# Moving the last tile's transposes into the first plain block, and fixing VectorE's order there, in a one-core diffusion layer

## The chip, the cores and the metric

The kernel runs on one core of a Trainium2 chip. The metric is the device time of one execution in microseconds (us). Before the change the median of three runs is 766.42 us (765.01 to 767.63). One core has a matrix engine (TensorE, "PE" in the profile; its weight loads are "PEld"), VectorE ("DVE"), ScalarE ("ACT"), GpSimd ("POOL") and SyncE ("SP"), which here only issues DMAs.

## What is computed

One layer of a hybrid backbone on 640 tokens: 128 context tokens and 512 latent tokens, model width 1024. Cut to what matters, for each of the two token kinds with its own conditioning vector:

```
mod = silu(cond) @ w_ada + b_ada           # six vectors: sh1, sc1, g1, sh2, sc2, g2
h   = rms(x) * (1 + sc1) + sh1
proj = h @ w_in                            # q, k, v and three conv inputs
mix = concat(rms(attention), rms(conv mixer)) @ w_out
x   = x + g1 * mix
h2  = rms(x) * (1 + sc2) + sh2             # <- the change is here
gate, up = split(h2 @ w_gate_up)           # 1024 -> 2 x 2816
x   = x + g2 * ((silu(gate) * up) @ w_down)
```

All is float32. Each float32 product is made of three matmuls in a faster format: an operand is split into a rounded part "hi" (a copy by ScalarE) and a remainder "lo" (a subtraction by VectorE), and hi·hi + hi·lo + lo·hi is accumulated.

## The kernel before

The tokens lie in five tiles of 128, in the order TORD: context, then latent tiles 0 to 3. TensorE's instructions run in program order (a manual schedule for that engine alone). The other engines' orders are made at build time by a greedy planner, which takes ready instructions by priority; a priority is the place in the program, moved ahead by `early(n)` or behind by a negative n. The order that it makes is then fixed on each engine's queue.

**Output projection** (lines 1040 to 1105). For each half j of the 1024 output columns, and each token tile, 24 matmuls into two PSUM accumulators, one for attention and one for the conv mixer. With j = 0 the tile's result gets its two row scales (L1079 on ScalarE, L1080 on VectorE), then is multiplied by g1 (L1082) and added to x (L1083); these two run on GpSimd for the first PX = 2 tiles, on VectorE for the others. ScalarE then squares the sum with accumulation along the row (L1095), and VectorE makes a mean (L1098). With j = 1 VectorE does the same work in four instructions (L1086 to L1090), and the second sum of squares completes the mean (L1101), GpSimd takes it to the power -1/2 (L1103), and VectorE writes the normalised tile x2n (L1105; one buffer). Beside it VectorE accumulates g2 from streamed weights (g2_step, "aacc", L989/L991), at low priority, and splits the weights of half 1 (L246 on ScalarE, L247 on VectorE). Weights come by SP's queue into three buffers "wf"; a load waits until the buffer's last reader is done.

**h2_turn(t)** (L953). Eight 128x128 transposes of x2n on TensorE (L960) into two PSUM tiles, then eight evictions with scale and shift into h2. The table H2E says how many of each four go to VectorE (L966); the others go to ScalarE (L968). For latent tile 3, the last, that is two of four. Tiles but the last are transposed inside the loop of j = 1, one tile late.

**Feed-forward.** The 22 column blocks f of w_gate_up: the first two are "plain", the others use a Strassen-like scheme with seven products in place of eight. The 640 tokens are two halves of 320, LO and HI, and h2 makes the quarters B11, B21 (LO) and B12, B22 (HI). The last tile is columns 192 to 320 of HI. A plain block on LO needs B11 and B21; on HI it needs B12 and B22. Blocks f = 2 on also need the token sums T1 to T4 (b_sums, L1028): each a subtraction of quarters (tr, L1035), ScalarE's copy (L1021) and VectorE's remainder (L1022). Before the change the order in the program is: B12 and B22 of columns 0 to 192, sums of columns 0 to 192, block 0 LO, the last tile's h2_turn, B12 and B22 of columns 192 to 320, block 1 LO, sums of columns 192 to 320, block 0 HI, block 1 HI.

**Operands of the weights** (op_load, L193). A block's g and u halves are loaded whole, and each quarter, or sum of quarters (sx, L205), is split by L149 (ScalarE) and L150 (VectorE) into a buffer "wh" or "wl", four of each, which is free again when TensorE has used it for the last time. W(key) loads up to nine entries ahead of the one that is asked for; entries of f = 2 and later have phase 3 and are held back until phase[0] is 3. Until then the stream ends with block 1's last operand.

Of the kernel before, what the change touches and what calls it, by code (L numbers as in the profile page):

```python
# [58 lines left out]
RSP = 0  # L59
G2P = -300  # L60
CRP = '0e'
H2E = [0, 0, 0, 2, 0]
PX = 2
SPO = 0
BHD = ("B21",)
TL = 1
# [3 lines left out]
PHB = 2  # L70
XP = [50, 400]
BP = 300
AP0 = 60
MXP = [300, 200, 0, 0, 0]
AWB = 2
# [14 lines left out]
def build(ctx, tc, x_prompt, x_sample, c, cache_k, cache_v, c_ctx, norm_mix, norm_ffn, w_ada, b_ada,  # L90
# [54 lines left out]
    def early(n):  # L145
        return tc.high_priority(n)
# [804 lines left out]
    TORD = [CTX] + list(range(NL))  # L951
    TS = {t: slice(n * P, (n + 1) * P) for n, t in enumerate(TORD)}

    def h2_turn(t):
        cc = 1 if t == CTX else 0
        for g in range(2):
            tp = PB((P, 4, P))
            for i in range(4):
                k = 4 * g + i
                pe.transpose(tp[:, i], x2n[t][:, k * P:(k + 1) * P], ident)  # L960
            for i in range(4):
              with early(BP):
                k = 4 * g + i
                dst, a, b = h2[g][:, i, TS[t]], modA[1][:, k, cc:cc + 1], modB[1][:, k, cc:cc + 1]
                if i >= 4 - H2E[t]:
                    dve.tensor_scalar(dst, tp[:, i], a, b, ALU.mult, ALU.add)  # L966
                else:
                    act.activation(dst, tp[:, i], AF.Identity, bias=b, scale=a)  # L968
# [71 lines left out]
    for j in range(2):  # L1040
        cols = slice(j * 512, (j + 1) * 512)
        for n, t in enumerate(TORD):
            cc = 1 if t == CTX else 0
            c0 = t * P + (2 if t == CTX else 0)
            if j == 0:
                with early(MXP[n]):
                    mixed[t] = [mix_ctx if t == CTX else mix_half(of[t]),
                                mix_half(yf[:, :, c0:c0 + P], "sx" if t == NL - 1 else "mx")]
            ms = mixed[t]
            ab = [PB(tag="h") for _ in range(2)]  # L1050
            for half in range(2):
                for p in range(4):
                    wh, wl = W(("o", j, 2 * half + p // 2))
                    mm3(ab[half], ms[half][0][:, p], ms[half][1][:, p], wh[:, p % 2], wl[:, p % 2],
                        p == 0, p == 3)
                if j == 0 and CRP == f"{n}{'me'[half]}":
                    next(ada_gen, None)
                    conv_rms()
            if j == 1 and n:
                h2_turn(TORD[n - 1])  # L1060
                with early(BP):
                    if n == 2:
                        b_plain("B11 B21", slice(0, 256))
                    if n == 3:
                        b_plain("B11 B21", slice(256, HALF))
            if j == 0 and n == 1:
                att_rms(NL - 1)
                act.activation(warm, rA[NL - 1], AF.Silu)
            if j == 0 and G2N <= n < 4 + G2N:
                g2_step(0, n - G2N)  # L1070
            if j == 1 and n == 0:
                g2_out(0)
            if j == 0:
                x2[t] = T("x2", (P, D), F32, NT)
                sp.dma_start(x2[t], x_dram[t])
            with early(XP[j]):
                m = T("mix", (P, 512), F32, 2)
                if j == 0:
                    act.activation(m, ab[0], AF.Copy, scale=rA[t])  # L1079
                    dve.scalar_tensor_tensor(m, ab[1], rB[t], m, ALU.mult, ALU.add)  # L1080
                    e = pool if n < PX else dve
                    e.tensor_tensor(m, m, g1[cc][:, cols], ALU.mult)  # L1082
                    e.tensor_tensor(x2[t][:, cols], m, x2[t][:, cols], ALU.add)  # L1083
                else:
                    with early(AP0):
                        dve.scalar_tensor_tensor(m, ab[0], rA[t], g1[cc][:, cols], ALU.mult, ALU.mult)  # L1086
                        dve.tensor_tensor(x2[t][:, cols], m, x2[t][:, cols], ALU.add)
                    m = T("mix", (P, 512), F32, 2)
                    dve.scalar_tensor_tensor(m, ab[1], rB[t], g1[cc][:, cols], ALU.mult, ALU.mult)
                    dve.tensor_tensor(x2[t][:, cols], m, x2[t][:, cols], ALU.add)  # L1090

            
            ss = T("ss", (P, 1), F32, 6)
            with early(XP[j]):
                act.activation(m, x2[t][:, cols], AF.Square, accum_out=ss)  # L1095
                if j == 0:
                    ms0[t] = T("ms0", (P, 1), F32, NT)
                    dve.tensor_scalar(ms0[t], ss, 1.0 / D, EPS, ALU.mult, ALU.add)  # L1098
                else:
                    q = T("ms", (P, 1), F32, 4)  # L1100
                    dve.tensor_scalar(q, ss, 1.0 / D, ms0[t], ALU.mult, ALU.add)  # L1101
                    r = T("rs", (P, 1), F32, 6)
                    pool.tensor_tensor(r, q, neghalf[:, :1], ALU.pow)  # L1103
                    x2n[t] = T("x2n", (P, D), F32, 1)
                    dve.tensor_scalar_mul(x2n[t], x2[t], r)  # L1105
# [16 lines left out]
        for k in range(4):  # L1122
            mm3(out[:, :HALF], w[:, 0, k], w[:, 1, k], *B[b][k], start and k == 0, stop and k == 3, more)

    def plain(f, bs, toks):

        ps = [FB(), FB()]
        for x, a in zip(ps, ("A1", "A2")):
            for i in (1, 2):
                prod(x, f, f"{a}{i}", bs[i - 1], i == 1, i == 2)  # L1130
        if toks is LO:
            st[f] = T("cg", (P, TOK), F32, 2), T("cu", (P, TOK), F32, 2)
        cg, cu = st[f]
        act.activation(cg[:, toks], ps[0][:, :HALF], AF.Silu)
        dve.tensor_tensor(cu[:, toks], ps[1][:, :HALF], cg[:, toks], ALU.mult)
        if toks is HI:
            ff_out(f, cu)
            del st[f]
# [97 lines left out]
    for gi, grp in enumerate(GROUPS):  # L1236
        for f in grp:
            if f == 0:
                two = slice(0, 192), slice(192, HALF)
                b_plain("B12 B22", two[0])  # L1240
                b_sums(two[0])
                for x in range(NPLAIN):
                    plain(x, ("B11", "B21"), LO)
                    if x == 0:
                        h2_turn(TORD[-1])
                        with early(BP):
                            b_plain("B12 B22", two[1])
                        phase[0] = 3
                b_sums(two[1])
                for x in range(NPLAIN):  # L1250
                    plain(x, ("B12", "B22"), HI)
            elif f >= NPLAIN:
                ff_a(f)
                if f - 1 in st and FEND == 1:
                    ff_end(f - 1)
                ff_c(f)
                if f - 1 in st:
                    ff_end(f - 1)
                ff_d(f)
                ff_b(f)  # L1260
                ff_e(f)
                if f == grp[-1] or FEND == 0:
                    ff_end(f)
# [55 lines left out]
```

## Time and profile before

| | us |
|---|---|
| median of three runs | 766.42 (765.01 to 767.63) |
| profiled execution, device time | 764.62 |
| its span | 762.8 |
| TensorE busy | 740.0 (97%) |
| VectorE busy | 558.8 (73%) |
| ScalarE busy | 368.8 (48%) |
| GpSimd busy | 48.9 (6%) |

The page has the busy time of each engine, the chain of work that ended last, and the costliest groups. A view of waits lists, for an engine, the line that waited, who released it, the total, the count and the longest. A timeline gives start, duration, engine, line, operation, output and inputs, shape and count of one or several merged instructions, and in brackets the idle time before and its releaser. A view by windows gives the busy time of each engine in a stretch and the TensorE clock that was granted (PEclk, 1.00 is full). Durations of neighbours overlap by pipelining. Phases of the span: input and q/k/v up to about 60 us, attention and conv to 252, output projection to 320, feed-forward to the end; within it, the plain blocks are at 321 to 356.

### The profile page before, as it was taken

To read this page: it belongs to the slowest core of one execution; us is meant where nothing else is said; L and a number is where in the kernel's file an instruction comes from. 1 tells how busy PE (TensorE), PEld (TensorE's weight loads), DVE (VectorE), ACT (ScalarE), POOL (GpSimd) and SP (SyncE) were. 2 spreads that over 40 slices of the span, in tenths; PEclk is the share of its full clock that TensorE was granted. 3 is DMA by queue.
4 is the path that set the end of the run, shared out by engine and by line. 5 is a ranking of instruction groups with operands and counts; after the bars stand their busy time and mean duration, and the time that the engine had idled before them with its cause. 6 is when DMAs were issued, how large, how long until landed. Compare 5 with 4: busy or idle time off the path is not lost.

```text
span 762.8 us, 11866 instructions
## 1 busy us (share of the span) xinstructions
PE 740.0 (97%) x4580; PEld 664.3 (87%) x4580; DVE 558.8 (73%) x1008; ACT 368.8 (48%) x711; POOL 48.9 (6%) x77
## 2 busy tenths in 40 slices
PE   4999999999999999989999999999999999999997
PEld 3678888989999876879998789998889998899986
DVE  5566987676666797888879678884578866788653
ACT  5355776666665534755552135553125541255410
POOL 3105201011010230000000000000000000000000
PEclk9999999999999999999999999999999999999999
DMA  9994134424425353031335313233113232222312
GB/s 292 303 245 132 46 107 141 123 91 125 138 90 166 119 186 111 1 111 56 93 101 175 88 56 110 70 98 111 55 56 103 64 111 77 62 85 82 111 55 83
DMA packets 102349, 84.52 MB, mean 111 GB/s; under 512 B 4526, under 2 KB 82674, under 8 KB 102292
## 3 DMA queue, kind: packets, MB, share of 16 engines
q1 hardware_dynamic: 100980, 83.39, 35.7%
q8 instruction: 36, 0.59, 0.3%
q10 hardware_dynamic: 1056, 0.26, 0.2%
q14 instruction: 21, 0.17, 0.1%
q0 software_dynamic: 256, 0.11, 0.1%
HBM read 79.68 MB, written 2.75 MB: 108 GB/s over the span
## 4 chain that ended last, share of the span: by engine, by line
PE 80%; DVE 9%; DMA 4%; issue 2%; ACT 2%; SPq 1%; POOL 1%; POOLq 0%; DVEq 0%; ACTq 0%
PE pf L153 17%; PE pf L154 17%; PE pf L155 17%; PE pc L676 3%; PE pc L677 3%; PE pc L678 3%; PE ps L790 2%; PE po L833 2%; PE pt L816 2%; PE pc L378 2%; DMA af<-in_w_ada_dram 2%; DMA wf<-in_w_gate_up_dram 1%; PE ps L153 1%; DVE aacc L991 1%; PE ph L154 1%
## 5 line engine op out<-in xcount | busy, mean ns | idle before, releaser
L149 ACT ACTIVATE wh<-wf 128x1024 fp32r<-128x1024 f32 (+1 forms) x76 | 64.1, 843 | 93.4 <-PE pf L155 63.1
L153 PE MATMUL pf<-wh,gT 128*128 128x512 f32 (+1 forms) x225 | 88.1, 392 | 0.0
L154 PE MATMUL pf<-wl,gT 128*128 128x512 f32 (+1 forms) x225 | 87.7, 390 | 0.0
L155 PE MATMUL pf<-wh,gT 128*128 128x512 f32 (+1 forms) x225 | 87.7, 390 | 0.0
L150 DVE TENSOR_TENSOR wl<-wf,wh 128x1024 fp32r<-128x1024 f32 (+1 forms) x42 | 49.4, 1175 | 28.2 <-ACT wh L149 25.3
L676 PE MATMUL pc<-hH,wh 128*128 128x320 f32 x192 | 61.1, 318 | 0.0
L677 PE MATMUL pc<-hL,wh 128*128 128x320 f32 x192 | 59.4, 310 | 0.0
L678 PE MATMUL pc<-hH,wl 128*128 128x320 f32 x192 | 59.3, 309 | 0.0
L153 PEld LDWEIGHTS pf<-wh,gT 128*128 128x128 f32 x225 | 42.2, 187 | 10.0 <-ACT wh L149 0.2
L154 PEld LDWEIGHTS pf<-wl,gT 128*128 128x128 f32 x225 | 42.2, 187 | 9.9 <-DVE wl L150 0.2
L155 PEld LDWEIGHTS pf<-wh,gT 128*128 128x128 f32 x225 | 42.2, 187 | 9.8
L153 PE MATMUL pf<-T,wh 128*128 128x320 f32 x160 | 49.6, 310 | 0.1
L154 PE MATMUL pf<-T,wl 128*128 128x320 f32 x160 | 49.5, 309 | 0.0
L155 PE MATMUL pf<-T,wh 128*128 128x320 f32 x160 | 49.5, 309 | 0.0
L154 PE MATMUL pf<-T,wh 128*128 128x320 f32 x160 | 49.5, 309 | 0.0
L155 PE MATMUL pf<-T,wl 128*128 128x320 f32 x160 | 49.5, 309 | 0.0
L153 PE MATMUL pf<-T,wl 128*128 128x320 f32 x160 | 49.5, 309 | 0.0
L153 PE MATMUL pf<-B,wl 128*128 128x320 f32 x152 | 47.3, 311 | 0.0
L154 PE MATMUL pf<-B,wl 128*128 128x320 f32 x152 | 47.1, 310 | 0.0
L155 PE MATMUL pf<-B,wl 128*128 128x320 f32 x152 | 47.1, 310 | 0.0
L1231 DVE TENSOR_TENSOR dm<-pf,g 128x512 f32<-128x512 f32 (+1 forms) x41 | 27.7, 674 | 22.9 <-PE pf L155 22.9
L149 ACT ACTIVATE wl<-wf 128x512 fp32r<-128x512 f32 x34 | 21.4, 629 | 44.7 <-PE pf L154 36.8
(297 smaller groups left out, 2052.3 us busy)
## 6 DMA issues: line engine op xcount, KB each, us to landing
wf<-in_w_gate_up_dram SPq DMA_DIRECT2D x44, 512.0 KB, 3.9
aw<-in_w_ada_dram SPq DMA_DIRECT2D x24, 512.0 KB, 4.9
wf<-in_w_down_dram SPq DMA_DIRECT2D x20, 512.0 KB, 3.4
wf<-in_w_in_dram SPq DMA_DIRECT2D x18, 512.0 KB, 5.9
af<-in_w_ada_dram SPq DMA_DIRECT2D x32, 256.0 KB, 6.0
x<-in_x_sample_dram SPq DMA_DIRECT2D x8, 512.0 KB, 4.4
wf<-in_w_out_dram SPq DMA_DIRECT2D x8, 512.0 KB, 4.6
wf<-in_w_ada_dram SPq DMA_DIRECT2D x8, 512.0 KB, 3.8
```

The costliest lines, as they stand in the source:

```text
L149: act.activation(hi, src, AF.Copy)
L150: dve.tensor_tensor(lo, src, f32(hi), ALU.subtract)
L153: pe.matmul(out, lh, rh, start=start, stop=False, skip_group_check=more)
L154: pe.matmul(out, lh, rl, start=False, stop=False, skip_group_check=more)
L155: pe.matmul(out, ll, rh, start=False, stop=stop, skip_group_check=more)
L378: pe.matmul(out[CG * g:CG * (g + 1)], cp[:, k], w, start=(k < 4), stop=(k >= KD - 4), skip_group_check=True)
L676: pe.matmul(acc, wh[:, k], hH[k][:, c0:c0 + n], start=(k == 0), stop=False)
L677: pe.matmul(acc, wh[:, k], hL[k][:, c0:c0 + n], start=False, stop=False)
L678: pe.matmul(acc, wl[:, k], hH[k][:, c0:c0 + n], start=False, stop=(k == KD - 1))
L790: pe.matmul(s2[:, g, :320], q, kk[:, v, P + g * 320:P + (g + 1) * 320], start=(i == 0), stop=(i == 1))
L816: pe.transpose(tp[:, i, h], u[3][h][:, kt * P:(kt + 1) * P], ident)
L1231: dve.tensor_tensor(dm, ps[:, :n], g2[cc][:, oc], ALU.mult)
```

## The change

- The last tile's h2_turn is called from inside plain block 0 LO, between its third and its fourth product (`mid`), with priority 1500 ahead for the evictions (BPL), and all eight evictions are on ScalarE (H2E all 0).
- B12 and B22 of columns 192 to 320 follow block 0 LO as before, with the same priority of 1500.
- The token sums are cut at column 128 in place of 192: columns 128 to 320, which hold the last tile, come first, behind the last tile's B copies; columns 0 to 128 come after block 1 LO.
- After the first part, four entries of the weight stream are loaded by hand: g and u of f = 2, its operand A11 and its operand S1. phase[0] becomes 3 only behind the second part of the sums.
- From B12/B22 of columns 0 to 192 to the second part of the sums, VectorE's instructions keep their order in the program (manual_schedule for DVE).
- PX = 0: multiply and add of the first two tiles of projection half 0 go from GpSimd to VectorE.
- The squares are taken with a scale of D^-0.5, so that the accumulated sum is the mean; L1098 falls away, and L1101 adds the two halves and epsilon.

```diff
-H2E = [0, 0, 0, 2, 0]
-PX = 2
+H2E = [0, 0, 0, 0, 0]
+PX = 0
+BPL = 1500
-    def h2_turn(t):
+    def h2_turn(t, first=None):
...
-              with early(BP):
+              with early(first or BP):
...
-            ss = T("ss", (P, 1), F32, 6)
+            ss = T("ss", (P, 1), F32, 6) if j else T("ssq", (P, 1), F32, NT)
             with early(XP[j]):
-                act.activation(m, x2[t][:, cols], AF.Square, accum_out=ss)
+                act.activation(m, x2[t][:, cols], AF.Square, scale=D ** -0.5, accum_out=ss)
                 if j == 0:
-                    ms0[t] = T("ms0", (P, 1), F32, NT)
-                    dve.tensor_scalar(ms0[t], ss, 1.0 / D, EPS, ALU.mult, ALU.add)
+                    ms0[t] = ss
                 else:
                     q = T("ms", (P, 1), F32, 4)
-                    dve.tensor_scalar(q, ss, 1.0 / D, ms0[t], ALU.mult, ALU.add)
+                    dve.tensor_scalar(q, ss, ms0[t], EPS, ALU.add, ALU.add)
...
-    def plain(f, bs, toks):
+    def plain(f, bs, toks, mid=None):
         ps = [FB(), FB()]
         for x, a in zip(ps, ("A1", "A2")):
             for i in (1, 2):
+                if mid is not None and (a, i) == ("A2", 2):
+                    mid()
                 prod(x, f, f"{a}{i}", bs[i - 1], i == 1, i == 2)
...
-                two = slice(0, 192), slice(192, HALF)
-                b_plain("B12 B22", two[0])
-                b_sums(two[0])
+                dve_order = tc.manual_schedule(engines={mybir.EngineType.DVE})
+                dve_order.__enter__()
+                b_plain("B12 B22", slice(0, 192))
                 for x in range(NPLAIN):
-                    plain(x, ("B11", "B21"), LO)
+                    plain(x, ("B11", "B21"), LO, None if x else lambda: h2_turn(TORD[-1], BPL))
                     if x == 0:
-                        h2_turn(TORD[-1])
-                        with early(BP):
-                            b_plain("B12 B22", two[1])
-                        phase[0] = 3
-                b_sums(two[1])
+                        with early(BPL):
+                            b_plain("B12 B22", slice(192, HALF))
+                        b_sums(slice(128, HALF))
+                        for _ in range(4):
+                            load_next()
+                b_sums(slice(0, 128))
+                dve_order.__exit__(None, None, None)
+                phase[0] = 3
                 for x in range(NPLAIN):
                     plain(x, ("B12", "B22"), HI)
```

## The prediction

> **What bounds the kernel now.** I read the page first, then TensorE's waits, then the timeline of each engine where a wait stands.
>
> ```profile
> span 762.8 us, 11866 instructions
> PE 740.0 (97%) x4580; PEld 664.3 (87%) x4580; DVE 558.8 (73%) x1008; ACT 368.8 (48%) x711; POOL 48.9 (6%) x77
> ...
> PE 80%; DVE 9%; DMA 4%; issue 2%; ACT 2%; SPq 1%; POOL 1%; POOLq 0%; DVEq 0%; ACTq 0%
> ```
>
> TensorE is busy for 97% and holds 80% of the chain that ended last. The change adds and takes no matmul, so it can only win where TensorE stands still or runs at a lower clock. Its waits, over the whole span, at the places that the diff touches:
>
> ```profile
> PE pf L153 <- ACT gT L1021: 3.1, 1, 3.1
> ...
> PE ph L154 <- DVE wl L247: 0.6, 2, 0.4
> ...
> PE ph L153 <- ACT wh L246: 0.5, 1, 0.5
> ...
> PE pf L154 <- DVE gT L1022: 0.3, 1, 0.3
> ```
>
> The first and the last belong to one place, the start of the second token half (HI) of the plain blocks. The middle two are in the output projection. TensorE's timeline at the first place:
>
> ```profile
> 321.30 0.40 PE L153 MATMUL pf<-B,wh 128*128 128x320 f32 x1
> ...
> 328.49 1.03 PE L960 MATMUL pt<-ident,x2n 128*128 128x128 f32 x8
> 329.28 0.40 PE L153 MATMUL pf<-B,wh 128*128 128x320 f32 x1
> ...
> 336.26 0.31 PE L155 MATMUL pf<-B,wl 128*128 128x320 f32 x1
> 339.68 0.41 PE L153 MATMUL pf<-gT,wh 128*128 128x320 f32 x1 [3.11 <-ACT gT L1021]
> ...
> 348.94 0.31 PE L153 MATMUL pf<-gT,wh 128*128 128x320 f32 x1
> ...
> 355.98 0.31 PE L153 MATMUL pf<-B,wh 128*128 128x320 f32 x1
> ...
> 357.74 0.31 PE L153 MATMUL pf<-T,wl 128*128 128x320 f32 x1
> ```
>
> Plain block 0 on the first half (LO) runs from 321.30 to 328.49 (7.19 us for four products of twelve matmuls, so 1.8 each), then come the last tile's eight transposes (0.79), then block 1 LO to about 336.4. Block 0 HI should start there; it starts at 339.68 and lasts until 348.94, which is 9.26 where its twin on the same half takes 355.98 - 348.94 = 7.04. The excess, 2.2, is a low clock beside the 0.3 wait:
>
> ```profile
> 336.41:339.68 3.27, 0.16 (x2) 0.00 (x1) 3.15 (x8) 2.92 (x8) 0.00 (x0) 1.00 0.00 0
> 339.68:344.00 4.32, 4.01 (x15) 3.78 (x16) 4.29 (x7) 1.45 (x3) 0.00 (x0) 0.60 0.00 0
> ```
>
> In these windows (length, then busy time of PE, PEld, DVE, ACT, POOL, then PEclk) TensorE stands for 3.27 us and is then granted 0.60 of its clock for 4.32 us: 0.40 x 4.32 = 1.7 lost. **The place costs 3.27 + 2.22 = 5.5 us.** What it waits for is B12 and B22 on the last tile's columns, and who is late for that stands in VectorE's timeline:
>
> ```profile
> 325.10 0.75 DVE L1105 TENSOR_SCALAR x2n<-x,rs 128x1024 f32<-128x1024 f32 x1 [0.44 <-POOL rs L1103]
> ...
> 329.91 0.95 DVE L1035 TENSOR_TENSOR tr<-gT 128x768 f32<-128x768 f32 x1
> 332.36 0.69 DVE L205 TENSOR_TENSOR sx<-wf 128x512 f32<-128x512 f32 x1 [1.50 <-DMA wf<-in_w_gate_up_dram]
> ...
> 333.84 0.95 DVE L1022 TENSOR_TENSOR T<-tr,T 128x768 fp32r<-128x768 f32 x1
> ...
> 338.18 1.36 DVE L966 TENSOR_SCALAR gT<-pt,modA,modB 128x128 f32<-128x128 f32 x4
> ...
> 341.14 0.68 DVE L1022 TENSOR_TENSOR B<-gT,B 128x512 fp32r<-128x512 f32 x1
> 342.74 0.68 DVE L1035 TENSOR_TENSOR tr<-gT 128x512 f32<-128x512 f32 x1
> ...
> 347.48 1.28 DVE L1022 TENSOR_TENSOR T<-tr,T 128x512 fp32r<-128x512 f32 x2
> ```
>
> The transposes are done by 329.3, but VectorE's half of the evictions runs at 338.18: ahead of it in VectorE's queue stand the first token sums (329.91 on) and an operand sum (sx) that waits 1.50 us for a weight. It is an order of work, not an amount.
>
> **The change, part by part.** *Transposes earlier.* They go behind three of block 0's four LO products: 321.30 + 3 x 1.8 = 326.7 instead of 328.49. The normalised tile x2n is written at 325.10 + 0.75 = 325.85, so they wait for nothing, with 0.85 us to spare; TensorE does the same work. Cost 0; if x2n slips by more than 0.85, the excess.
>
> *All eight evictions on ScalarE, then the B copies.* ScalarE's rows:
>
> ```profile
> 323.45 1.83 ACT L968 ACTIVATE gT<-pt,modB,modA 128x128 f32<-128x128 f32 x5
> ...
> 330.89 0.85 ACT L1021 ACTIVATE T<-tr 128x768 fp32r<-128x768 f32 x1 [2.47 <-DVE tr L1035]
> ...
> 339.63 0.63 ACT L1021 ACTIVATE B<-gT 128x512 fp32r<-128x512 f32 x1
> ```
>
> Eight at 1.83 / 5 = 0.37 are 2.9, then two copies of 0.63: from 327.2 to about 331.5, and 1.3 later if two splits of weights (0.65 each) stand in front. VectorE's fixed order there is: two 768-wide B remainders, three weight remainders of block 1, block 0's product (which needs the end of block 0 LO, 329.3), then the two 512-wide B remainders. With 0.95, 0.68 and 0.48 us each from 326.97 on (where the first stands before), it reaches the last two at about 331.4 and ends them at 332.8, at worst 334.1. TensorE asks for them at 336.4. So **the stall goes, and with it the low clock: -5.5**, with 2 to 3.5 us to spare.
>
> The clock could be weighed otherwise. The Trainium skill ("TensorE: Matmul & The Clock Gate", "Part 1: The HAM clock gate") says that the clock falls after an idle window of about 3.4 us whose phase is not tied to the kernel. By that, a gap of 3.27 would only sometimes lower the clock and the place would be worth 3.6 in such runs; in this trace the 3.27 us gap did lower it.
>
> *Token sums, now behind the last tile and in a fixed order.* Each of the four sums is a subtraction, ScalarE's copy, a second subtraction; written out, VectorE waits for the copy each time: 0.95 + 0.85 + 0.95 = 2.8 at 192 columns, 0.68 + 0.63 + 0.68 = 2.0 at 128. From 332.8: first part to 344.0. Behind it stand the four forced loads: two transfers on SP's queue (g and u of f=2), A11's remainder, and S1's sum, copy and remainder, 0.7 + 0.7 + 0.65 + 0.7 = 2.7. Their buffers of hi/lo operands come free with block 0 HI's first two products, at 336.4 + 3.6 = 340.0, so no wait. Then block 1's LO product (0.5), 347.2, and the second part: T1 ready at 349.2, T2 351.2, T3 353.2, T4 355.2. TensorE without the stall reaches block f=2 at 355.98 - 5.5 = 350.5, S1.T1 at 352.2 (1.76 later by the two rows above), S2.T2 at 354.0, S3.T3 at 357.5, A22.T4 at 359.3. Least slack 2.8 us, so cost 0; cover gone, each us late is a us of TensorE.
>
> *The weight of f=2's u* now starts behind block 1's A12 remainder, which stands behind both B remainders (about 329.5 instead of 327.13):
>
> ```profile
> 327.13 5.21 DMA wf<-in_w_gate_up_dram
> ```
>
> It lands near 334.7 and S1 is built after 344: nothing. Later transfers on SP's queue keep their order. What is late next is f=3's operands, a rival below.
>
> *GpSimd free (PX = 0).* For the first two tiles of projection half 0, multiply and add move to VectorE:
>
> ```profile
> 267.30 1.58 POOL L1082 TENSOR_TENSOR mix<-mix,g 128x512 f32<-128x512 f32 x1 [0.93 <-DVE mix L1080]
> 268.95 1.62 POOL L1083 TENSOR_TENSOR x<-mix,x 128x512 f32<-128x512 f32 x1
> ```
> ```profile
> 280.23 0.69 DVE L1082 TENSOR_TENSOR mix<-mix,g 128x512 f32<-128x512 f32 x1
> 280.95 0.69 DVE L1083 TENSOR_TENSOR x<-mix,x 128x512 f32<-128x512 f32 x1
> ```
> ```profile
> L991 DVE SCALAR_TENSOR_TENSOR aacc<-wf,cs,aacc x14: 732/740/1780, 258.4 to 278.6; 128x512 f32<-128x512 f32 x14
> ```
>
> VectorE takes 4 x 0.69 = 2.8 more. But its accumulations (aacc), 0.74 each at the median, take up to 1.78 while GpSimd runs: 1.04 lost for each of the four GpSimd instructions, 4.2 in all. Net -1.4 for VectorE, and each tile's chain is 1.8 shorter. That matters for TensorE's second stall:
>
> ```profile
> 279.82 0.40 PE L153 MATMUL ph<-wh,mx 128*128 128x512 f32 x1
> ...
> 285.43 0.40 PE L153 MATMUL ph<-wh,m 128*128 128x512 f32 x1
> ...
> 293.47 1.88 PE L999 MATMUL pt<-aacc,ones 128*128 128x512 f32 x4
> ```
>
> A tile's 24 matmuls take 5.61 (279.82 to 285.43), the next tile's take 8.04: **2.4 lost**, by the waits for L246/L247, the splits of half 1's output weights, which stand in both queues behind these tiles' chains. Bounds: -2.4 (all of it) to +2.8 (VectorE only gets longer). The contention row and the shorter chain lie near the first end; I take -1.4, VectorE's own net.
>
> *Squares scaled in the activation, five tiny VectorE instructions gone.* Short ones beside others; 0.
>
> *Allowance* for a queue order that I can't see: +0.3.
>
> **Sum:** -5.5 - 1.4 + 0.3 = -6.6. The profiled execution took 764.62 (span 762.8 and 1.82 around it): 758.0. It lies 1.8 under the median of the runs shown, 766.42, so for the median I say **759.8**.
>
> **Rivals.** *A, the projection gets worse:* VectorE's 2.8 lands in front of the L247 splits, the stall grows to 5.2. For it: VectorE is nearly gapless from 266 to 293; against: the contention row. 766.4 - 5.5 + 2.8 = 763.7; unchanged, 760.9.
>
> *B, the lead is eaten:* f=3's S1 is split at
>
> ```profile
> 360.29 0.69 DVE L150 TENSOR_TENSOR wh<-sx,wh 128x512 fp32r<-128x512 f32 x1
> ```
>
> and used eight products behind 355.98, at 370.1: a lead of 9.1. TensorE comes 5.5 earlier and the sums end 355.2 - 348.8 = 6.4 later, so a lead of -2.8 if VectorE's waits in the fixed order (0.63 to 0.85 each, eight times) stay empty, about +3 if f=2's operands fill them. Against it: the four evictions and the 1.50 us wait are gone from that queue. 759.8 + 2.8 = 762.6.
>
> *C, a shorter gap stays:* x2n or the B copies slip past their slack of 0.85 and 2 us by one or two instructions, say 1 us, with the low clock as now: 759.8 + 1 + 1.7 = 762.5.
>
> *D, the change doesn't do what it says:* the weight splits, not the evictions, hold the queue, and HI starts as late as before; only the projection gains: 766.4 - 1.4 = 765.0.
>
> *E, slower:* one mechanism, the head of VectorE's fixed order. T2 is the sixth round; if each copy waits on ScalarE behind x us of other work, TensorE waits 6x - 2.8 at S2.T2. From x = 0.5 on it costs; at x = 1.9, three instructions of 0.63 in front of every copy, it is 8.6, with 1.7 of low clock 10.3: 759.8 + 10.3 = 770.1. Break-even is at x = 1.3. Against it: before, the T copy starts at 330.89, within 0.1 of its input, and ScalarE is busy 48%.
>
> **How the numbers follow.** Forecast 0.49, A 0.12, B 0.12, C 0.10, D 0.08, E 0.09. About 0.3% (2.3 us) can be told from no change: faster is below 764.1. The forecast and most of A, B, C lie there: 0.79; D and the rest 0.12; E 0.09. Range: the low end is both places won in full (-7.9) with runs 1 us lower, 757.5; the high end takes A, B, C and D in, 765.2.
>
> **What would show it.** Right: TensorE's waits lose the 3.1 at L153 and the granted clock stays 1.00 after it; the last tile's L968 come as eight in a row within 5 us of the transposes; aacc's maximum falls to 0.74; the 24 matmuls behind 285 take near 5.6. Wrong: a new TensorE wait for T (L1022), for an operand remainder (L150) at f=2 or f=3, for x2n at L960, or a longer one for L247. Each would name its rival.

## The result, and the profile after

The changed kernel takes 759.65 us (median of five runs, 759.29 to 762.66) where the kernel before, run beside it, takes 766.42 (765.01 to 767.63). The ratio is 0.9927, with a 95% interval of 0.99 to 0.9953. The forecast was 759.8 with a range of 757.5 to 765.2, and "faster". The profiled execution after took 762.66, the slowest of the five.

The page of the kernel after, answering to the lines shown of before (span, busy times, the shares of the chain that ended last):

```profile
span 760.9 us, 11844 instructions
...
PE 739.5 (97%) x4580; PEld 664.6 (87%) x4580; DVE 552.7 (73%) x1003; ACT 369.6 (49%) x715; POOL 43.1 (6%) x73
...
PE 82%; DVE 8%; DMA 3%; ACT 2%; SPq 2%; issue 1%; POOL 1%; DVEq 0%; POOLq 0%
```

TensorE's waits of the kernel after, from the stage that the diff touches on (line, releaser, total, count, longest):

```profile
PE pf L154 <- DVE cu L1183: 1.5, 1, 1.5
...
PE pf L154 <- ACT u L1154: 0.5, 1, 0.5
```

The four waits of before (3.1 and 0.3 at the start of HI, 0.5 and 0.6 in the output projection) are gone, and two new ones of 2.0 in all have come. (Most line numbers behind the edits are one or two higher than before; L1101 to L1105 keep theirs.) TensorE's timeline of the kernel after shows where they stand:

```profile
265.23 0.47 PE L154 MATMUL ph<-wh,mx 128*128 128x512 f32 x1
...
288.68 0.39 PE L154 MATMUL ph<-wh,m 128*128 128x512 f32 x1
...
294.29 1.88 PE L1000 MATMUL pt<-aacc,ones 128*128 128x512 f32 x4
...
322.11 0.40 PE L154 MATMUL pf<-B,wh 128*128 128x320 f32 x1
...
327.54 1.03 PE L961 MATMUL pt<-ident,x2n 128*128 128x128 f32 x8
...
337.21 0.31 PE L154 MATMUL pf<-gT,wh 128*128 128x320 f32 x1
...
351.29 0.31 PE L154 MATMUL pf<-B,wh 128*128 128x320 f32 x1
353.05 0.31 PE L154 MATMUL pf<-T,wl 128*128 128x320 f32 x1
...
354.98 0.41 PE L154 MATMUL pf<-T,wh 128*128 128x320 f32 x1
...
359.28 0.42 PE L154 MATMUL pf<-T,wh 128*128 128x320 f32 x1 [0.51 <-ACT u L1154]
...
364.54 0.41 PE L154 MATMUL pf<-B,wh 128*128 128x320 f32 x1 [1.47 <-DVE cu L1183]
...
424.68 1.88 PE L1000 MATMUL pt<-cg,ones 128*128 128x512 f32 x4
```

The 24 matmuls behind 288.68 take 5.61 where they took 8.04. Block 0 HI starts at 337.21 without a gap, and lasts as long as its twin (337.21 to 351.29 is 14.08 for both). The new waits are in block f = 2, at its third and its fourth sum product, behind 351.29.

From such rows each kernel's span can be cut into stages, so that a run's time is compared place by place. The start is everything up to the first matmul of the second token tile in the output projection (261.98 before, 265.23 after). **P** goes from there to the first matmul on aacc (293.47 before, 294.29 after). Then come 27.8 us that are the same in every run, up to block 0 LO. **H** goes from block 0 LO to the start of f = 2 (321.30 to 355.98 before, 322.11 to 351.29 after). **F** goes from there to the matmul on the accumulator of g2's second half (its tile is called cg), 424.68 after, where 16 blocks are still to come; the rest is 336.15 to 336.24 in every run. TensorE's timeline of the kernel before has that matmul at

```profile
426.65 1.88 PE L999 MATMUL pt<-cg,ones 128*128 128x512 f32 x4
```

"Behind the start" is P to the end, and the ratio by stages is 766.42 plus the change of that column, over 766.42.

| kernel | start | P | H | F | behind the start | ratio by stages | ratio of times (95%) | median, us |
|---|---|---|---|---|---|---|---|---|
| before | 261.98 | 31.49 | 34.68 | 70.67 | 500.82 | 1 | 1 | 766.42 |
| after | 265.23 | 29.06 | 29.18 | 73.39 | 495.67 | 0.9933 | 0.9927 (0.99 to 0.9953) | 759.65 |
| e1_gpsimd_back | 264.52 | 31.38 | 29.18 | 72.97 | 497.58 | 0.9958 | 0.9958 (0.9945 to 0.997) | 762.75 |
| e2_gpsimd_only | 266.16 | 29.05 | 34.34 | 70.81 | 498.24 | 0.9966 | 0.9964 (0.9948 to 0.9981) | 763.75 |
| e3_free_order | 263.02 | 29.05 | 29.18 | 73.47 | 495.68 | 0.9933 | 0.9936 (0.9918 to 0.9954) | 761.16 |
| e5_transposes_after | 263.38 | 29.06 | 29.18 | 75.11 | 497.32 | 0.9954 | 0.9944 (0.9927 to 0.9962) | 761.59 |
| e8_no_forced_loads | 265.17 | 29.06 | 29.18 | 73.97 | 496.23 | 0.9940 | 0.9927 (0.9901 to 0.9954) | 760.86 |
| e7_copy_twice | 263.30 | 29.06 | 30.82 | 74.88 | 498.80 | 0.9974 | 0.9988 (0.9976 to 1.0) | 764.43 |
| e6_evict_vector | 261.87 | 29.06 | 29.18 | 72.53 | 494.83 | 0.9922 | 0.9922 (0.9902 to 0.9941) | 759.37 |
| e4_pipelined | 262.14 | 29.06 | 29.18 | 72.13 | 494.36 | 0.9916 | 0.9908 (0.9889 to 0.9927) | 759.28 |
| e11_split_behind_copy | 261.97 | 29.06 | 29.18 | 72.01 | 494.23 | 0.9914 | 0.9906 (0.989 to 0.9921) | 758.44 |
| e14_evict_pipe | 264.27 | 29.05 | 29.18 | 71.50 | 493.73 | 0.9907 | 0.9897 (0.9875 to 0.9918) | 757.93 |
| e13_evict_pipe_copy | 262.07 | 29.06 | 29.18 | 71.56 | 493.83 | 0.9909 | 0.9901 (0.988 to 0.9921) | 758.74 |

P takes two values, to 0.1 us. H is 34.68 and 34.34 in the two kernels with the old order of the sums and 29.18 in the others, e7_copy_twice aside. F is less steady: e1_gpsimd_back has the same order of instructions there as the kernel after on TensorE, VectorE and ScalarE, and takes 0.42 less, so smaller differences of F say little. The two columns of ratios agree in nearly every row. The start varies by up to 4.3 us from profile to profile, so spans alone don't compare. Read this way the change won 2.43 in P and 5.50 in H, and gave back **2.72 in F**: 5.15 in all behind the start.

### The profile page after: what moved, and what is told of

It reads as the page before. It is cut to its first block, busy times and chain, and to the rows that moved or that the text cites. A ratio compares the mean times of both kernels' runs of the same rounds, so it can differ in the third digit from the quotient of the medians.

```text
span 760.9 us, 11844 instructions
## 1 busy us (share of the span) xinstructions
PE 739.5 (97%) x4580; PEld 664.6 (87%) x4580; DVE 552.7 (73%) x1003; ACT 369.6 (49%) x715; POOL 43.1 (6%) x73
## 4 chain that ended last, share of the span: by engine, by line
PE 82%; DVE 8%; DMA 3%; ACT 2%; SPq 2%; issue 1%; POOL 1%; DVEq 0%; POOLq 0%
PE pf L154 17%; PE pf L156 16%; PE pf L155 16%; PE pc L677 3%; PE pc L678 3%; PE pc L679 3%; PE po L834 3%; PE ps L791 2%; PE ph L154 2%; PE pt L817 2%; PE ph L155 2%; PE ph L156 2%; PE pc L379 2%; DMA af<-in_w_ada_dram 2%; DMA wf<-in_w_gate_up_dram 1%
## 5 line engine op out<-in xcount | busy, mean ns | idle before, releaser
L154 PE MATMUL pf<-B,wh 128*128 128x320 f32 x136 | 42.3, 311 | 1.5 <-DVE cu L1183 1.5
```

The lines of the kernel that those rows point to most:

```text
L154: pe.matmul(out, lh, rh, start=start, stop=False, skip_group_check=more)
```

## The experiments

The sum had no loss in F beyond an allowance of 0.3. So the first runs split the change into its parts, and the later ones look for what F costs. All but e2_gpsimd_only are edits of the kernel after; all compute the same.

**GpSimd alone, taken back and alone.** e1_gpsimd_back is the kernel after with

```diff
-PX = 0
+PX = 2
```

and e2_gpsimd_only the kernel before with

```diff
-PX = 2
+PX = 0
```

> The changed kernel with multiply and add of the first two projection tiles back on GpSimd (PX = 2), nothing else. Three stages are read: P, from the second token tile's first matmul of projection half 0 to the first ones-by-aacc matmul (31.5 us before, 29.1 changed); H, from plain block 0 LO to block f=2 (34.7 before, 29.2 changed); F, from f=2 to the second ones-by-accumulator matmul (70.7 before, 73.4 changed). My theory (GpSimd slows VectorE's accumulations and lengthens the tiles' chains, so the splits of half 1's weights come late): P 31.5 again, H 29.2, F 73.4, time 2.4 us over the changed kernel, 762.1; aacc maximum 1.78 us again. Rival (the five tiny instructions or a reshuffled order elsewhere made the gain): P stays 29.1, time 759.7.

> The kernel before with PX = 0 alone. My theory: P 29.1 instead of 31.5, H 34.7 and F 70.7 as before, time 766.4 - 2.4 = 764.0. Rival (VectorE's 2.8 us more work counts): P 31.5 or more, up to 34, time 766.4 to 769.

Measured: P 31.38 with GpSimd back and 29.05 with it free, whatever else is changed. The group of the accumulations on VectorE (minimum, median and longest in ns), kernel after and then e1_gpsimd_back:

```profile
L992 DVE SCALAR_TENSOR_TENSOR aacc<-wf,cs,aacc x14: 735/747/752, 261.6 to 281.3; 128x512 f32<-128x512 f32 x14
```
```profile
L992 DVE SCALAR_TENSOR_TENSOR aacc<-wf,cs,aacc x14: 734/740/1777, 260.9 to 281.0; 128x512 f32<-128x512 f32 x14
```

and TensorE's timeline of e1_gpsimd_back:

```profile
293.23 0.49 PE L154 MATMUL ph<-wh,mx 128*128 128x512 f32 x1 [0.50 <-ACT wh L247]
```

With GpSimd in use the longest accumulation is 1.78 again and TensorE waits again for the splits of half 1's weights. So this part is worth 2.3 to 2.4 alone in P, all of the stall, as expected. The two runs don't say how that divides between the accumulations and the shorter chain of a tile. The Trainium skill ("SBUF — State Buffer", "Who interferes with whom") says that a VectorE instruction with two SBUF inputs contends with a GpSimd instruction that reads SBUF; the 1.78 that comes and goes with GpSimd agrees.

In e2_gpsimd_only HI still waits, for a little less (TensorE's timeline, then the window behind the wait: length, busy time of PE, PEld, DVE, ACT and POOL, then PEclk):

```profile
341.08 0.41 PE L153 MATMUL pf<-gT,wh 128*128 128x320 f32 x1 [2.78 <-ACT gT L1021]
```
```profile
341.08:345.00 3.92, 3.60 (x16) 3.38 (x17) 3.89 (x7) 1.05 (x3) 0.00 (x0) 0.73 0.00 0
```

**The transposes behind block 0 again.**

```diff
-                    plain(x, ("B11", "B21"), LO, None if x else lambda: h2_turn(TORD[-1], BPL))
+                    plain(x, ("B11", "B21"), LO)
                     if x == 0:
+                        h2_turn(TORD[-1], BPL)
```

> The changed kernel with the last tile's transposes behind plain block 0 LO again, as before the change; evictions on ScalarE, B copies, order of VectorE as changed. H is now counted from block 0 LO to block f=2 (34.7 before, 29.2 changed), F from there to the second ones-by-accumulator matmul (70.7 before, 73.4 changed). My theory (the place of the transposes was not what held the B copies; there is slack of 2 to 3 us): transposes 1.8 later, B remainders done about 1 us later and still ahead of TensorE, H 29.2, no wait at the start of block 0 HI; F 73.4 to 74.5 as the sums start later. Rival (the earlier transposes made the gain): a wait of TensorE for L1023 and H 31 or more, with the low clock behind it.

Measured: H stays 29.18, so the 5.5 of HI don't need the earlier transposes. But F is 75.11, 1.72 worse than after, and more than the 73.4 to 74.5 expected. In TensorE's timeline of e5_transposes_after, and in its window behind, the fourth sum product of f = 2 waits twice as long as in the kernel after, and the clock falls:

```profile
363.21 0.39 PE L154 MATMUL pf<-B,wh 128*128 128x320 f32 x1 [3.05 <-DVE cu L1183]
```
```profile
363.20:366.70 3.50, 3.49 (x16) 3.50 (x17) 2.50 (x6) 0.82 (x3) 0.00 (x0) 0.65 0.48 141
```

A delay of the last tile ahead of the sums is thus paid at f = 2, in F, and not at HI. Most of the 1.72 is the clock: by the distances between starts of matmuls, this one gap makes TensorE 3.3 late where all those of the kernel after make it 3.1, and the other 1.5 is the stretch of low clock behind it.

**What makes VectorE late at f = 2.** VectorE's timeline of the kernel after, from the last tile on:

```profile
325.90 0.75 DVE L1105 TENSOR_SCALAR x2n<-x,rs 128x1024 f32<-128x1024 f32 x1 [0.44 <-POOL rs L1103]
...
333.06 0.69 DVE L1023 TENSOR_TENSOR gT<-gT,gT 128x512 fp32r<-128x512 f32 x1 [1.86 <-ACT gT L1022]
333.67 0.69 DVE L1023 TENSOR_TENSOR B<-gT,B 128x512 fp32r<-128x512 f32 x1
334.27 0.95 DVE L1036 TENSOR_TENSOR tr<-gT 128x768 f32<-128x768 f32 x1
336.13 0.96 DVE L1023 TENSOR_TENSOR T<-tr,T 128x768 fp32r<-128x768 f32 x1 [0.91 <-ACT T L1022]
...
352.65 0.68 DVE L1023 TENSOR_TENSOR T<-tr,T 128x512 fp32r<-128x512 f32 x1
...
357.05 0.69 DVE L1023 TENSOR_TENSOR T<-tr,T 128x512 fp32r<-128x512 f32 x1
357.65 0.48 DVE L1137 TENSOR_TENSOR cu<-pf,cg 128x320 f32<-128x320 f32 x1
...
364.00 0.48 DVE L1183 TENSOR_TENSOR cu<-pf,u 128x320 f32<-128x320 f32 x1
```

It stands idle for 1.86 in front of the last tile's two B remainders, while ScalarE evicts, and 0.91 in each of the four first rounds (a round is the subtraction, copy and remainder of one sum). From 345.2 to 367.3 it has no idle time at all, since the sums' second part, the operands of f = 2 and the products of the blocks all want it. The last remainder ends at 357.74, where it was 348.76 before the change. What is late then is not a T but the work of the blocks themselves. ScalarE's timeline of the kernel after shows how it gets to TensorE:

```profile
329.62 2.89 ACT L969 ACTIVATE gT<-pt,modB,modA 128x128 f32<-128x128 f32 x8
...
358.17 0.74 ACT L150 ACTIVATE gT<-cu 128x640 fp32r<-128x640 f32 x1 [0.36 <-DVE cu L1137]
358.81 0.42 ACT L1154 ACTIVATE u<-pf 128x320 f32<-128x320 f32 x1
```

The copy of a product out of PSUM (u, L1154) stands behind the split of block 1's output, which waits for VectorE's product (L1137, 357.65). TensorE wants that PSUM buffer at 358.8 and gets it at 359.28: the 0.51. Later VectorE's own product cu (L1183) comes only at 364.00, and TensorE waits 1.47 for it.

**Is it the fixed order?** e3_free_order leaves the manual schedule of VectorE away and changes nothing else.

```diff
-                dve_order = tc.manual_schedule(engines={mybir.EngineType.DVE})
-                dve_order.__enter__()
...
-                dve_order.__exit__(None, None, None)
```

> The changed kernel without VectorE's fixed order; the planner orders VectorE, all else as changed. My theory (evictions on ScalarE with the long lead free the B copies, the fixed order only costs the waits for ScalarE's copies): H 29.2 to 30, F near 70.7, time 757 to 758. Rival (only the fixed order keeps the B remainders ahead of the sums and weight remainders): H 31 to 35, with a wait of TensorE for L1023 and a low clock, time 762 to 766.

Measured: H is 29.18, so with the rest of the change in place the planner too has the B copies ready for HI. F is 73.47 where 70.7 was expected: the same loss as after, so "the fixed order costs it" falls. The planner makes VectorE wait elsewhere (VectorE's, then TensorE's timeline of e3_free_order):

```profile
330.45 0.69 DVE L206 TENSOR_TENSOR sx<-wf 128x512 f32<-128x512 f32 x1 [1.87 <-DMA wf<-in_w_gate_up_dram]
```
```profile
354.36 0.42 PE L154 MATMUL pf<-T,wh 128*128 128x320 f32 x1 [1.61 <-ACT p L1154]
```

An operand sum that waits 1.87 for a weight is put ahead of the token sums, and TensorE waits 1.61 for a PSUM copy at f = 2. It is the same pattern: ScalarE's copy p starts at 353.89, behind the split of block 1's output (353.25), which waits for VectorE's product (352.73). But here the sums aren't late: the last remainder ends 27.82 us after the start of block 0 LO, 27.46 before and 35.63 after, and VectorE's idle time from block 0 LO to f = 2 is 2.3, as before (2.2; 5.9 after). So late sums aren't needed for the loss. What both orders share is that TensorE comes to f = 2 5.5 us earlier than before, counted from block 0 LO, while VectorE's work for it gains less: in e3_free_order the product that holds up copy p starts 32.8 us after block 0 LO, and 36.9 before the change, so it comes 4.0 earlier. The 1.5 between is nearly the wait. What TensorE's earlier arrival costs by itself no run separates.

**The forced loads.** e8_no_forced_loads takes the four load_next() away.

```diff
-                        for _ in range(4):
-                            load_next()
```

> The changed kernel without the four entries loaded by hand behind the first part of the sums; the weights and operands of f=2 then come with block HI, and the planner sets them into VectorE's waits: two operand sums now stand ahead of block 0's product and the last B remainders, and wait for the weight of f=2's u. My theory (what TensorE pays at f=2 is VectorE's empty time in the rounds, us for us): the rounds are filled in part, F 72 to 73 (73.4 changed, 70.7 before), H 29.2 if that weight lands in time, up to 30.5 if not. Rival (the late phase and loads make f=2 late): F over 74.

Measured: F 73.97. It was expected at 72 to 73, and this missed: without the operands built between the two parts, f = 2 is 0.6 worse, and TensorE waits 1.79 for copy p and 1.38 for cu. The loads aren't the cause. Whether they help is not certain, with 0.6 of difference in F and the same ratio of times as after.

**ScalarE's copy of each sum done twice.**

```diff
-            act.activation(w[:, 0, :, part], src, AF.Copy)
+            for _ in range(2 if name[0] == "T" else 1): act.activation(w[:, 0, :, part], src, AF.Copy)
```

> The changed kernel with ScalarE's copy of each token sum made twice, the second over the first, so that each of the eight rounds of the fixed order gets longer by about 0.75 (first four) and 0.55 us (last four, where other work fills the gap in part). My theory (VectorE's lag at f=2 comes from these rounds, and TensorE pays for it): the first four rounds end 3.0 us later, T2 some 4 us later; H 29.2, F 73.4 + 2.5 to 4.5 = 76 to 78, time 762.5 to 764. Rival (the rounds have slack and the lag comes from elsewhere): F 73.4 to 74.

Measured: H + F is 105.70 against 102.57, 3.1 longer. H is longer here only because the start of f = 2 is read as 1.76 ahead of its first product on a T, which waits (TensorE's timeline of e7_copy_twice):

```profile
352.76 0.41 PE L154 MATMUL pf<-T,wl 128*128 128x320 f32 x1 [1.48 <-ACT T L1022]
353.88 0.41 PE L155 MATMUL pf<-T,wl 128*128 128x320 f32 x1 [0.71 <-DVE T L1023]
...
356.90 0.41 PE L155 MATMUL pf<-T,wh 128*128 128x320 f32 x1 [0.67 <-DVE T L1023]
```

In the kernel after T2 is done at 352.65 + 0.68 = 353.33 and asked for at 354.98, 1.65 of slack. Six copies more, four of 0.85 and two of 0.63, are 4.7, and 4.7 - 1.65 = 3.0; the three waits for T1 and T2, 1.48, 0.71 and 0.67, are 2.9. That is the price of rival E's mechanism, in this one run one us of TensorE for each us by which the rounds outrun the slack. The change as made doesn't reach it.

**Filling the waits of the rounds.** In e4_pipelined each sum's subtraction is issued ahead of the remainder of the sum before it, so that VectorE doesn't stand while ScalarE copies.

```diff
             dve.tensor_tensor(w, y, z, ALU.subtract)
-            b_put(x, w, part)
+            if held: b_put(*held)
+            held = x, w, part
...
+        b_put(*held)
```

> The changed kernel with the token sums' program order turned so that each subtraction stands ahead of the remainder of the sum before it (tr1, tr2, T1, tr3, T2, tr4, T3, T4); the fixed order of VectorE then has something to do while ScalarE copies. My theory (the eight waits of 0.9 and 0.6 us for ScalarE's copy made VectorE late at f=2, which gave TensorE's two waits of 0.5 and 1.5 us): the 0.91 us gaps at L1023 go, both waits go, F 70.7 to 71.3, time 757.0 to 757.6. Rival (the forced loads and the late phase made f=2's operands late): F stays near 73.4, time 759.7.

Measured: F 72.13, so 1.26 of the 2.72 comes back; 70.7 to 71.3 was expected, and that missed. VectorE's timeline of e4_pipelined has no idle time in the rounds, as meant:

```profile
332.16 0.96 DVE L1036 TENSOR_TENSOR tr<-gT,tr 128x768 f32<-128x768 f32 x1
333.04 0.96 DVE L1023 TENSOR_TENSOR T<-tr,T 128x768 fp32r<-128x768 f32 x1
```

A wait is left, in ScalarE's and then TensorE's timeline of e4_pipelined:

```profile
351.49 0.74 ACT L150 ACTIVATE gT<-cu 128x640 fp32r<-128x640 f32 x1 [0.37 <-DVE cu L1138]
352.13 0.42 ACT L1155 ACTIVATE p<-pf 128x320 f32<-128x320 f32 x1
```
```profile
352.61 0.41 PE L154 MATMUL pf<-T,wh 128*128 128x320 f32 x1 [0.72 <-ACT p L1155]
```

It is the same pattern one step earlier: the PSUM copy p behind a split that waits for VectorE's product.

**That split moved behind the copy.** e11_split_behind_copy is e4_pipelined with block 1's output split (ff_out) held until f = 2's copy p is issued.

```diff
         if toks is HI:
-            ff_out(f, cu)
+            held_out.append((f, cu)) if f == NPLAIN - 1 else ff_out(f, cu)
...
-        st[f] = [b1, copy_of("p1", b1), cg, None, None, None, None]
+        order_act = tc.manual_schedule(engines={mybir.EngineType.Activation}) if held_out else ExitStack()
+        with order_act:
+            p1 = copy_of("p1", b1)
+            if held_out: ff_out(*held_out.pop())
+        st[f] = [b1, p1, cg, None, None, None, None]
```

> The kernel with the pipelined sums (F 72.1, of which one wait of 0.72 us for ScalarE's copy p of block f=2's first product), with one swap on ScalarE: the hi copy of block 1's output (gT, which waits for VectorE's product of block 1 HI) stands behind that copy p in place of ahead of it. My theory (ScalarE's queue hands VectorE's lag on to TensorE: the copy is ready but stands behind an instruction that waits for VectorE): the wait at S2.T2 goes, F 71.2 to 71.4, time about 0.8 us under the pipelined kernel. Rival (the copy itself or its input is late): F stays 72.1, the wait stays.

Measured: F 72.01, where 71.2 to 71.4 was expected. The wait for p is gone, and another has come (ScalarE's, VectorE's and TensorE's timeline of e11_split_behind_copy):

```profile
354.63 0.63 ACT L150 ACTIVATE wh<-sx 128x512 fp32r<-128x512 f32 x1 [2.58 <-DVE sx L206]
```
```profile
353.85 0.69 DVE L206 TENSOR_TENSOR sx<-wf 128x512 f32<-128x512 f32 x1 [0.63 <-DMA wf<-in_w_gate_up_dram]
```
```profile
356.39 0.41 PE L154 MATMUL pf<-T,wh 128*128 128x320 f32 x1 [1.15 <-ACT u L1157]
```

The next PSUM copy (u) now stands behind an operand split that waits 2.58 for VectorE, which itself waits for a weight of f = 3. Moving this one ScalarE instruction only moved the wait on.

**VectorE evicts half again.** e6_evict_vector is the kernel after with the old table of evictions, within the fixed order.

```diff
-H2E = [0, 0, 0, 0, 0]
+H2E = [0, 0, 0, 2, 0]
```

> The changed kernel with half of the last tile's evictions on VectorE again (H2E 2 for that tile), inside its fixed order. My theory (it was the place in VectorE's order that was late, not the engine): the four stand ahead of the sums now, H 29.2, F 73 to 74.5. Rival (VectorE can't evict in time beside its other work): TensorE waits for L1023 at block 0 HI, H 31 to 35.

Measured: H 29.18, so the evictions needn't be on ScalarE for HI. F is 72.53, 0.86 better than with ScalarE alone; 73 to 74.5 was expected, and this missed. VectorE's and TensorE's timeline of e6_evict_vector, and its window behind the wait:

```profile
327.36 1.36 DVE L967 TENSOR_SCALAR gT<-pt,modA,modB 128x128 f32<-128x128 f32 x4
...
329.64 0.69 DVE L1023 TENSOR_TENSOR B<-gT,B 128x512 fp32r<-128x512 f32 x1
```
```profile
360.64 0.42 PE L154 MATMUL pf<-B,wh 128*128 128x320 f32 x1 [1.98 <-DVE cu L1183]
```
```profile
360.60:364.00 3.40, 3.36 (x23) 3.37 (x24) 3.16 (x6) 1.40 (x3) 0.00 (x0) 1.00 0.45 133
```

The 1.36 of evictions fit into the 1.86 in which VectorE would have waited for ScalarE's. The last B remainder ends at 330.33; moved by the difference of the starts (265.23 - 261.87 = 3.36) that is 333.69, against 334.36 after, so the sums begin 0.67 earlier.

**Both together.** e14_evict_pipe joins the edits of e4_pipelined and e6_evict_vector; e13_evict_pipe_copy adds to these the held split of e11_split_behind_copy, and a higher priority for the products of the plain blocks:

```diff
-        dve.tensor_tensor(cu[:, toks], ps[1][:, :HALF], cg[:, toks], ALU.mult)
+        with early(400): dve.tensor_tensor(cu[:, toks], ps[1][:, :HALF], cg[:, toks], ALU.mult)
```

> The changed kernel with the pipelined sums (F 72.1 alone) and with half of the last tile's evictions on VectorE (F 72.5 alone), where VectorE else waits 1.9 us for ScalarE's copies. My theory (VectorE's lag is handed to TensorE about us for us until f=3's weight transfer, released by f=2's last operand, sets the limit): the sums end 0.8 earlier, F 71.3 to 71.8, H 29.2. Rival (with the rounds filled the lag no longer decides): F 72.1.

> As the one with both, and besides the output products of the plain blocks with priority on VectorE and the hi copy of block 1's output behind ScalarE's copy p. My theory: F 70.8 to 71.3, stages from the second tile on 4 to 5 us shorter than before plus 2.4 of the projection, time 757.0 to 758.0, the fastest of all. Rival (the wait only goes on to the next copy): F as without these two, 71.3 to 72.

Measured: F 71.50 with the two edits, as expected, 1.9 less than after, and one wait is left in TensorE's waits of e14_evict_pipe behind the projection:

```profile
PE pf L154 <- ACT u L1155: 0.5, 1, 0.5
```

With the rest added F is 71.56, where 70.8 to 71.3 was expected, and this missed: nothing more is won, and the wait for the next copy u is 0.92. e14_evict_pipe is the fastest kernel run: 757.93 us (757.38 to 759.81), 1.94 behind the start and 1.7 in the medians under the kernel after. The intervals of the two ratios to the kernel before overlap, so by times alone the gain over the change as made is likely and not certain; by stages it is there.

## Why the prediction was right, and where it was not

**Right, by its own steps.** *The HI stall, -5.5*: H fell by 5.50. The last tile's evictions are eight in a row at 329.62 (2.89 where 2.9 was worked out), the B remainders end at 334.36 and TensorE asks at 337.21: a slack of 2.85 in the 2 to 3.5 given. Block 0 starts 0.81 later in this profile than in that of before, so 334.36 is 333.55 on the prediction's scale, between 332.8 and 334.1. The low clock went with the stall (kernel after, window from the start of HI):

```profile
337.00:347.00 10.00, 10.00 (x70) 10.00 (x69) 7.26 (x11) 3.83 (x6) 0.00 (x0) 1.00 0.00 0
```

*Transposes at no cost*: x2n is done at 326.65, 0.89 ahead of its first transpose, 0.85 was worked out. HI didn't need their move, as e5_transposes_after shows; it pays in F, by 1.7, most of it the clock. *The rounds*: 2.74 each with 0.91 of idle in them, 2.8 was worked out; T2 comes 1.65 ahead of its product, 2.8 was worked out, and no T is waited for, though the last sum ends 1.7 later than worked out (357.74 is 356.9 on the prediction's scale, where 355.2 stood). *The weight of u*: no wait for it appears.

**Mis-sized: GpSimd, -1.4.** P fell by 2.43, the whole stall, which was the lower bound. The mechanism was right (aacc's maximum falls from 1.780 to 0.752, and the 24 matmuls take 5.61). VectorE's own net was the wrong measure: the stall hung on the splits behind the chains of these tiles, and it is gone as a whole.

**Failed: "Least slack 2.8 us, so cost 0".** The step compared each T with the product that uses it, and there it held. It left out everything else that f = 2 needs of VectorE, while TensorE comes 5.5 us earlier: the products of the blocks, the operand sums, and the copies on ScalarE that stand behind splits of these products. In the kernel after, the sums put that work back further: the last remainder ends 9.0 us later than before (357.74 against 348.76; 8.2 if the later start is taken off). In e3_free_order it isn't later, and F is lost all the same, so the sums are not the whole cause. The two waits that show in the kernel after are 2.0 of the 2.72 lost in F. The other 0.7 is lateness that the profile counts as busy time (71.35 in F against 70.53 before): these matmuls are given 0.31 each and start 0.15 apart, so the first 0.16 of a wait lies under the matmul ahead of it. By their starts, four matmuls of F come 0.17, 0.67, 1.63 and 0.22 late (354.98, 359.28, 364.54, 377.18) and the one behind each 0.1 more, 3.1 in all; before there is one such place, of 0.4. Rival B named the mechanism, VectorE without idle time behind the sums, and "what is late next is f = 3's operands"; its size came near (+2.8), though worked out for another place: the loss stands at f = 2, in PSUM copies and products. Within the fixed order, the time that VectorE's first part takes sets the size of the loss, as e4_pipelined, e6_evict_vector and e7_copy_twice show: with 0.91 a round taken out F falls, with 1.36 of eviction put into a gap it falls, with the copies doubled H + F grows.

**The sum, then**, is -5.5 - 2.43 + 2.72 = -5.2 where -6.6 stood. The median fell by 6.77 and hit the forecast by 0.15 us. That is closer than the reasoning was, and in part luck: two terms were off in opposite directions, by 1.0 and 2.7, and the medians fell 1.6 further than the stages. The interval of the ratio, 3.6 to 7.7 us, holds both sums, and the start, which the change doesn't touch, moves single profiles by more than their difference.

**The other rivals.** A: no, P is shorter. C: no, no gap stayed at HI. D: no, H fell by all of the 5.5. But none of the three things that the step named is needed by itself: HI keeps no stall with the transposes late (e5_transposes_after), with VectorE evicting half (e6_evict_vector) or without the fixed order (e3_free_order). What these runs share is the program's order, with the sums behind the last tile's B copies, and the higher priority of evictions and B copies (BPL); neither was taken away alone, so which of them removes the stall stays open. On VectorE itself the order needn't be strict: in e3_free_order two subtractions of the sums run ahead of the last tile's B remainders, the first of which ends at 334.62, 0.37 ahead of block 0 HI. E: no, a copy starts as soon as its input is done (the first at 335.26, where the subtraction ends at 335.22), and T2 keeps 1.65; the experiment with doubled copies has its price.

## What to carry to other kernels

When a stall is removed by putting one engine's work in order, follow that engine until it has idle time again, not only to the consumer of what was moved: here no T came late, and the loss stood behind them, in PSUM copies and products queued behind the sums. In a chain that goes between two engines (subtract, copy, subtract), issue the next step's first half ahead of this step's second, and let an engine do in its own wait what another is late with: these two edits won back 1.9 of 2.7. Cut the span into stages at fixed instructions before comparing profiles.

## What the runs showed of the hardware that was not expected

**Which gaps lower the clock.** In the plain blocks and in f = 2, gaps of TensorE of 3.11 (before), 3.05 (e5_transposes_after) and 2.78 us (e2_gpsimd_only) were followed by a low clock. Gaps of 1.98 (e6_evict_vector), 1.79 (e8_no_forced_loads), 1.61 (e3_free_order) and 1.47 (kernel after) left it at 1.00; the window behind the last of these:

```profile
364.50:368.00 3.50, 3.46 (x23) 3.47 (x24) 3.27 (x7) 1.15 (x2) 0.00 (x0) 1.00 0.25 72
```

The low clock was the same each time, 0.50 for 3.41 us: from 340.56 to 343.97 before, from 342.88 to 346.29 in e2_gpsimd_only, from 364.23 to 367.64 in e5_transposes_after. Half of 3.41 is 1.7 us of a busy TensorE. The 0.60, 0.73 and 0.65 that the windows give are means over stretches that hold all or a part of it; in e2_gpsimd_only the rest lies in the next window:

```profile
345.00:348.00 3.00, 3.00 (x19) 3.00 (x18) 3.00 (x6) 1.86 (x4) 0.00 (x0) 0.78 0.00 0
```

The length of one gap doesn't decide it everywhere: in e14_evict_pipe the clock is low from 75.68 to 79.09, and no gap between 34 and 75 us is longer than 1.07. The Trainium skill ("TensorE: Matmul & The Clock Gate", "Part 1: The HAM clock gate") puts it at an idle window of about 3.4 us; three gaps shorter than that lowered the clock in these runs, and the measurement decides. For this change the clock is 1.7 of the 5.5 that the HI stall was worth.

**The start.** It took from 261.87 to 266.16 in thirteen profiles, though up to the projection the order of the instructions on every engine is the same before and after. Part of it shows as clock and idle time in the input stage (40 to 50 us, kernel before and then after; the seventh number is PEclk):

```profile
40.00:50.00 10.00, 10.00 (x70) 7.45 (x74) 5.09 (x14) 3.57 (x5) 0.00 (x0) 1.00 1.10 302
```
```profile
40.00:50.00 10.00, 8.48 (x53) 6.08 (x50) 5.71 (x15) 4.66 (x6) 0.00 (x0) 0.83 1.04 285
```

The number of such stretches of 3.41 us at 0.50 in the first 100 us goes with it: four profiles with three of them (the kernel after is one) have starts of 264.52 to 266.16, the nine with at most two (before has one) 261.87 to 264.27. What decides how many there are was not tried.
